# Five edits to a one-core hybrid-attention layer: later decays, a full-row decay product, spread x loads, a GpSimd subtract, and a shorter last layer norm

## The chip, the cores and the metric

The kernel runs on one core of a Trainium2 chip. The metric is the device time of one execution in microseconds (us), the median over several runs.

## What is computed

One residual block on x of 2048 tokens by 1024 channels, fp32:

```python
IN_SIZES = (DN_WIDTH, DN_WIDTH, DN_WIDTH,     # q, k, v of branch A, 4 heads of 128
            DN_WIDTH,                         # its gate z
            DN_HEADS, DN_HEADS,               # beta and decay, one per head and token
            SWA_WIDTH, SWA_KV_WIDTH, SWA_KV_WIDTH, SWA_WIDTH,   # branch B: 8 query heads, 2 kv heads of 64
            D_MODEL, D_MODEL)                 # the two merge gates
# A: S <- exp(g_t) S;  S <- S + k_t (beta_t (v_t - S^T k_t))^T;  o_t = S^T q_t   (gated delta rule)
g = jnp.cumsum(g, axis=-1)
decay = jnp.where(causal, jnp.exp(jnp.where(causal, g[..., :, None] - g[..., None, :], 0.0)), 0.0)
t_inv = lax.linalg.triangular_solve(eye + lower, eye)     # lower = strict(k_beta k^T * decay)
```

Branch B is attention over a window of 128 tokens with learned sinks and partial rotary embedding. Each branch is gated and projected to 1024 channels, the two are merged by sigmoid gates computed from x, projected once more, added to alpha times x, and normalized: (r - mean) * rsqrt(var + eps) * weight + bias.

## The kernel before, in words

The 2048 tokens go in 4 chunks of T = 512, one after the other. All dense products are fp32 made of two halves: `split` (L148) and `load_x` (L210) take a raw tile `w` from memory, ACT writes its rounded half hi (L160, L218) and DVE the rest lo = raw - hi (L161, L219), and `prods` issues three matmuls per product (L179, L180, L181). A split weight is used in all four chunks: chunk 0 splits it and SP writes the pair to a scratch tensor `kw_...` (`keep`, L145); later chunks load the pair (`wb<-kw_...`, L156). Two rings matter: the raw tiles `w` are three (W_RAW), shared by weights and x, and the pairs `wb` are four (W_SPLIT). x of a chunk lives in eight hi and eight lo tiles (`px`), which the last gate product of a chunk reads; the next chunk's x goes into the same tiles.

The first weights and x of chunk 0 have their own path in `start` (L224): ACT splits x (L235), DVE makes its lo (L236), and DVE casts each of six weight tiles (L241) and subtracts (L242).

Per chunk and head, branch A runs as generators that are put between the dense products: `decays` (per chunk: gates on DVE, two cumulative sums by matmul, L293 and L294, and a transpose of them whose result `GT` (8 rows by 512) ACT writes, L310), then `front` per head: a transpose of k (L369), the product that spreads head h's decay to 128 rows (L382, an 8-row selector `sel` against `GT`), the product k k^T (L393). Its masked blocks go to memory (`scrm`) and come back as `su`; `inverse` (L427) inverts 32 by 32 blocks on DVE (L943, L944), writes the result `xi` to `scrp` (L432), and `levels` (L434) reads it back in four loads into `p_` (L445), which PE needs at L457, then L464 after a transpose on DVE (L450). `back` (L482) runs the recurrence: L504, DVE L506, L509 and L512, DVE L511, L515 and L517, four times per head. Attention scores are L598 and L599; its query rows L606 to L616 lie on DVE and ACT.

PE's order is written out at build time by class `Order` (L829): `spawn(name, task, after)` lets a generator start `after` ns of counted PE work later, and each `yield cost, latency` puts its next step behind that much more. `decays` is spawned with LAT_Y = 8300 once the window's keys are through (L270). The other engines' queues are ordered by a scheduler that estimates when each operand is ready; so a change in PE's order also changes the order of SP's DMA issues and of DVE. Each queue runs strictly in its order.

After the dense list of a chunk comes `branch_b` for eight output tiles d (L653), each with a half weight `b{d}`, and ahead of it one call `load_x(nxt, KT - 1)` issues all eight x loads of the next chunk. After the last chunk `last_project` (L734) computes 128 tokens at a time; the norm of the last 128 tokens is the end of the program: `norm_factors` (L693), then per half of 512 channels a scale and shift (DVE L764 or ACT L762), a weight (DVE L765), a bias (POOL L766 for the first half, DVE L766 for the second), and the output DMA (L767).

Of the kernel before, what the change touches and what calls it, by code (L numbers as in the profile page):

```python
# [8 lines left out]
F32 = mybir.dt.float32  # L9
F32R = mybir.dt.float32r  # L10
AF = mybir.ActivationFunctionType
ALU = mybir.AluOpType
# [4 lines left out]
P = 128  # L17
D = 1024
KT = D // P
T = 512  # L20
NB = T // P
NH = 4
# [14 lines left out]

PE_R, PE_F, PE_T, PE_Q = 216, 218, 109, 45

LAT_INV, LAT_B, LAT_S, LAT_N, LAT_SM, LAT_D, LAT_M, LAT_K, LAT_Q, LAT_Y, LAT_F, LAT_W = 29600, 2700, 2300, 7700, 9200, 11000, 9000, 1400, 7900, 8300, 4100, 2300  # L40
FIRST = ("h01", "h00", "h02")


# [20 lines left out]
def build(tc, xt, xn, wk, wg, par, lnp, cst, out, seq=2048):  # L64
    nc = tc.nc
    NCH = seq // T
    with ExitStack() as ctx:
# [64 lines left out]

        selt = const.tile([8, NH], F32, name="selt")
        nc.sync.dma_start(out=selt, in_=cst[:8, C_SEL:C_SEL + NH])
        sel = const.tile([8, NH], F32R, name="sel")
        nc.vector.tensor_copy(sel, selt)
        ctx.enter_context(tc.manual_schedule(engines={mybir.EngineType.PE}))


# [83 lines left out]
        def start(c):  # L223

            ps = [pp.tile([P, T], F32, name="pp") for _ in range(2)] + [pd.tile([P, T], F32, name="pd")]

            idle = mm.tile([P, T], F32, name="mm")
            for _ in range(WARM):
                nc.tensor.matmul(idle, S[:, 0], S.rearrange("p h d -> p (h d)"), start=True, stop=True)
            for k in range(KT):  # L230
                if not k % 2:
                    hi, lo = (px.tile([P, 2, T], F32R, name=n) for n in ("xh", "xl"))
                    c.xh += [hi[:, 0], hi[:, 1]]
                    c.xl += [lo[:, 0], lo[:, 1]]
                nc.scalar.activation(c.xh[k], first[f"x{k}"], AF.Copy)  # L235
                nc.vector.tensor_tensor(c.xl[k], first[f"x{k}"], c.xh[k].bitcast(F32), ALU.subtract)  # L236
                if not k % 4:
                    wb = [pw.tile([P, 2, 528], F32R, name="wb", bufs=W_SPLIT)[:, :, :512] for _ in FIRST]
                    wh, wl = ([b[:, n] for b in wb] for n in range(2))
                    for i in range(3):  # L240
                        nc.vector.tensor_copy(wh[i], first[i + 3 * (k // 4)])  # L241
                        nc.vector.tensor_tensor(wl[i], first[i + 3 * (k // 4)], wh[i].bitcast(F32), ALU.subtract)  # L242
                        keep((FIRST[i], k // 4), wb[i])
                for i in range(3):
                    sl = slice(128 * (k % 4), 128 * (k % 4) + 128)
                    yield from prods(ps[i], [(wh[i][:, sl], wl[i][:, sl], c.xh[k], c.xl[k])], k == 0, k == KT - 1)
            for i, j in enumerate((1, 0, 2)):
                conv_silu(c, j, 0, ps[i])
            st.spawn("front0", front(c, 0), LAT_F)
# [35 lines left out]
        def decays(c, ba):  # L285
            c.beta, c.g = gates_small(nc, sm, ba, nea, prm[:, P_DTB:P_DTB + 4])
            flat = lambda a: a.rearrange("p b h -> p (b h)")
            new = lambda name: sm.tile([P, NB, NH], F32, name=name)
            c.nG, c.kd, c.neG, c.eGl = new("nG"), new("kd"), new("neG"), new("eGl")
            psg = pd.tile([P, T], F32, name="pd")  # L290
            tri = sm.tile([P, P], F32, name="wc", bufs=1)
            nc.vector.tensor_scalar(tri, dmask, 0.0, None, ALU.is_ge)
            nc.tensor.matmul(psg[:, :16], tri, flat(c.g), start=True, stop=True)  # L293
            nc.tensor.matmul(psg[:, 16:32], ones, flat(c.g), start=True, stop=True)  # L294
            G = psg[:, :16].rearrange("p (b h) -> p b h", h=NH)
            gg = sm.tile([P, NB, 2, NH], F32R, name="ghl", bufs=1)
            nc.vector.tensor_copy(gg[:, :, 0], G)
            nc.vector.tensor_tensor(gg[:, :, 1], G, gg[:, :, 0].bitcast(F32), ALU.subtract)
            nc.vector.tensor_scalar(flat(c.nG), psg[:, :16], -1.0, None, ALU.mult)
            nc.vector.tensor_tensor(flat(c.kd), psg[:, 16:32], flat(c.nG), ALU.add)  # L300
            nc.scalar.activation(c.kd, c.kd, AF.Exp)
            nc.scalar.activation(c.neG, c.nG, AF.Exp, scale=-1.0)
            nc.vector.tensor_scalar(c.neG, c.neG, -1.0, None, ALU.mult)
            nc.scalar.activation(flat(c.eGl), psg[:, 16:32], AF.Exp)
            yield 2 * 426, 2000
            psr = pd.tile([P, T], F32, name="pd")
            for b in range(NB):
                nc.tensor.transpose(tok(psr, b)[:8], gg[:, b].bitcast(F32).rearrange("p a h -> p (a h)"), ident)
            c.GT = sm.tile([8, T], F32R, name="GT", bufs=1)
            nc.scalar.activation(c.GT, psr[:8], AF.Copy)  # L310
            yield 4 * PE_T, 1000

        def conv_silu(c, j, h, ps):
# [42 lines left out]
        def front(c, h):  # L356
# [22 lines left out]
            yield 4 * PE_T, LAT_B  # L379

            psR = p4()
            nc.tensor.matmul(psR, sel[:, h:h + 1].to_broadcast([8, P]), c.GT, start=True, stop=True)  # L382
            dt = t4("dt", 2)
            for b in range(NB):
                nc.vector.scalar_tensor_tensor(dt[:, b], psR[:, b], c.nG[:, b, h:h + 1], dmask, ALU.add, ALU.add)
# [304 lines left out]
            for bp in range(2):  # L690
                nc.vector.scalar_tensor_tensor(c.ra[bp][:, :, es], xr[bp], 2.0 * ALPHA, pss[bp], ALU.mult, ALU.add)

        def norm_factors(c, bst, bufs=None):  # L693
            mv = sm.tile([P, 2], F32, name="mv", bufs=NB)
            nc.vector.bn_aggr(mv, bst)
            va = sm.tile([P, 1], F32, name="va")
            nc.vector.tensor_scalar(va, mv[:, 1:2], 4.0e-5, None, ALU.add)
            rs = sm.tile([P, 1], F32, name="rs", bufs=NB)
            rsqrt(nc, sm, rs, va, mhalf)
            if bufs:  # L700
                return rs, mv[:, 0:1]
            nm = sm.tile([P, 1], F32, name="lnm")
            nc.vector.scalar_tensor_tensor(nm, mv[:, 0:1], -1.0, rs, ALU.mult, ALU.mult)
            return rs, nm

        def layer_norm(c):
            fs = []
            for b in range(NB):
                r = c.ra[b // 2][:, b % 2]
                bst = sm.tile([P, 4, 6], F32, name="st", bufs=1)[:, :2]  # L710
                for i in range(2):
                    nc.vector.bn_stats(bst[:, i], r[:, 512 * i:512 * i + 512])
                rs, mu = norm_factors(c, bst, NB)
                fs.append((r, rs, mu))
                yield None, 2500
            for eg in range(4):
                es = slice(256 * eg, 256 * eg + 256)
                lg = pa.tile([P, 2, 256], F32, name="s")
                nc.sync.dma_start(out=lg, in_=bass.AP(tensor=lnp.tensor, offset=lnp.offset + 256 * eg, ap=[[0, P], [D, 2], [1, 256]]))
                for r, rs, mu in fs:  # L720
                    nc.vector.scalar_tensor_tensor(r[:, es], r[:, es], mu, lg[:, 0], ALU.subtract, ALU.mult)
                    nc.vector.scalar_tensor_tensor(r[:, es], r[:, es], rs, lg[:, 1], ALU.mult, ALU.add)
                    yield None, 1800
            for bp in range(2):
                t0 = c.i * T + bp * 256
                nc.sync.dma_start(out=out[t0:t0 + 256].rearrange("(b p) e -> p b e", p=P), in_=c.ra[bp])
# [7 lines left out]
        def last_project(c):  # L734
# [9 lines left out]
            for b in range(NB):  # L744
                r, t0 = ra[b // 2][:, b % 2], c.i * T + b * P
                bst = sm.tile([P, 4, 6], F32, name="st", bufs=1)
                for e0 in (0, 2):
# [7 lines left out]
                    for e, ps in enumerate(pss):  # L755
                        es = slice(256 * (e0 + e), 256 * (e0 + e) + 256)
                        nc.vector.scalar_tensor_tensor(r[:, es], xr[:, e], 2.0 * ALPHA, ps, ALU.mult, ALU.add)
                        nc.vector.bn_stats(bst[:, e0 + e], r[:, es])
                rs, nm = norm_factors(c, bst)
                for hs in (slice(0, 512), slice(512, D)):  # L760
                    if hs.start:
                        nc.scalar.activation(r[:, hs], r[:, hs], AF.Identity, scale=rs, bias=nm)  # L762
                    else:
                        nc.vector.tensor_scalar(r[:, hs], r[:, hs], rs, nm, ALU.mult, ALU.add)  # L764
                    nc.vector.tensor_tensor(r[:, hs], r[:, hs], lg[:, 0, hs], ALU.mult)  # L765
                    (nc.vector if hs.start else nc.gpsimd).tensor_tensor(r[:, hs], r[:, hs], lg[:, 1, hs], ALU.add)  # L766
                    nc.sync.dma_start(out=out[t0:t0 + P, hs], in_=r[:, hs])  # L767

        class Chunk:
# [26 lines left out]
        for i in range(NCH):  # L796
# [7 lines left out]
                    piece(c, w)  # L804
            for name in ("window0", "window1"):
                st.finish(name)
            if i < NCH - 1:
                load_x(nxt, KT - 1)
            for d in range(KT):
                st.dense([branch_b(c, d)])  # L810
            if i < NCH - 1:
                for w, first_done in EARLY:
                    st.finish(first_done)
                    if w == "q0":
                        st.done -= early_done - {"decay", "kT0", "kT1", "kT2", "kT3"}
                    nxt.early.add(w)
                    piece(nxt, w)
# [202 lines left out]
```

## Time and profile before

| | us |
|---|---|
| median of 3 runs (1693.77 to 1695.6) | 1695.29 |
| the profiled execution | 1688.99 |
| its span | 1687.2 |
| PE busy | 1619.6 (96%) |
| DVE busy | 976.0 (58%) |
| ACT busy | 600.8 (36%) |
| POOL busy | 88.9 (5%) |

The profiled execution is 6.3 us under the median and has 1.8 us around its span. PE is at work almost all the time, so time can be lost only where PE waits, where a matmul takes longer than it must, or where the granted clock of PE is below 1.00 (0.50 is the lower of its two levels, 1.2 GHz of 2.4). Waits of other engines count only if PE stands behind them. Later times are counted from the start of the span.

### The profile page before, as it was taken

How to read it: one execution, taken by the hardware profiler on the slowest of the kernel's cores; microseconds unless marked ns; L12 is line 12 of the kernel's file. 1: busy time of each engine (PE TensorE's matmuls, PEld its weight loads, DVE VectorE, ACT ScalarE, POOL GpSimd, SP SyncE). 2: the span in 40 equal slices, each digit the busy share in tenths (PEclk: the TensorE clock that was granted, in tenths of full speed). 3: DMA queues.
4: the chain of work that ended last, by engine and by line, in shares of the span. 5: the costliest groups of instructions: out<-in, count | busy, mean ns of one | idle time of the engine just before them, and what ended most of it. 6: DMA issues, size and time to landing. Idle time of an engine off the chain costs nothing.

```text
span 1687.2 us, 26971 instructions
## 1 busy us (share of the span) xinstructions
PE 1619.6 (96%) x9846; PEld 1366.6 (81%) x9846; DVE 976.0 (58%) x3015; ACT 600.8 (36%) x1692; POOL 88.9 (5%) x138
## 2 busy tenths in 40 slices
PE   9999999899899999999999999999999999999997
PEld 6878877787788778788888778878888878888787
DVE  6676686548748665433746774623482867462255
ACT  4464456424313633432311453333230244233110
POOL 0100000000001001000000000000000100000001
PEclk9999999999989999999999999999999999999999
DMA  8866584676857446556655835645656664464862
GB/s 307 265 223 198 180 272 154 207 237 218 280 199 221 133 145 176 157 146 224 197 178 182 245 120 150 178 144 176 207 176 193 221 185 122 149 197 138 285 207 76
DMA packets 189157, 323.37 MB, mean 192 GB/s; under 512 B 31072, under 2 KB 45408, under 8 KB 188896
## 3 DMA queue, kind: packets, MB, share of 16 engines
q1 hardware_dynamic: 185184, 316.40, 59.3%
q0 software_dynamic: 3840, 5.25, 1.5%
q8 instruction: 78, 1.28, 0.3%
q14 instruction: 55, 0.45, 0.1%
HBM read 244.97 MB, written 71.37 MB: 187 GB/s over the span
## 4 chain that ended last, share of the span: by engine, by line
PE 79%; DMA 8%; DVE 8%; ACT 2%; issue 1%; SPq 1%; POOL 0%; DVEq 0%; ACTq 0%
PE mm L179 22%; PE mm L181 21%; PE mm L180 21%; PE pp L633 2%; DMA s<-in_lnp 2%; PE pp L625 1%; DMA wb<-kw_o 1%; DMA w<-in_wg 1%; DMA wb<-kw_zb 1%; PE pp L598 1%; PE pd L509 1%; PE pd L504 1%; PE pd L393 1%; PE pp L599 1%; DMA wb<-kw_b 1%
## 5 line engine op out<-in xcount | busy, mean ns | idle before, releaser
L179 PE MATMUL mm<-xh,wb 128*128 128x512 f32 x1128 | 467.1, 414 | 2.0 <-DMA wb<-kw_zb 1.6
L181 PE MATMUL mm<-xh,wb 128*128 128x512 f32 x1128 | 445.4, 395 | 0.0
L180 PE MATMUL mm<-xl,wb 128*128 128x512 f32 x1128 | 444.2, 394 | 0.0
L179 PEld LDWEIGHTS mm<-xh,wb 128*128 128x128 f32 x1128 | 213.1, 189 | 50.3 <-issue 8.9
L181 PEld LDWEIGHTS mm<-xh,wb 128*128 128x128 f32 x1128 | 212.3, 188 | 49.9
L180 PEld LDWEIGHTS mm<-xl,wb 128*128 128x128 f32 x1128 | 213.8, 190 | 38.0
L179 PE MATMUL mm<-wb,xh 128*128 128x256 f32 (+1 forms) x384 | 115.1, 300 | 3.2 <-DVE rope L893 2.9
L179 PE MATMUL mm<-wb,s 128*128 128x256 f32 x384 | 112.1, 292 | 5.5 <-DMA wb<-kw_o 5.3
L180 PE MATMUL mm<-wb,xh 128*128 128x256 f32 (+1 forms) x384 | 109.1, 284 | 0.0
L181 PE MATMUL mm<-wb,s 128*128 128x256 f32 x384 | 109.0, 284 | 0.0
L180 PE MATMUL mm<-wb,s 128*128 128x256 f32 x384 | 108.9, 284 | 0.0
L181 PE MATMUL mm<-wb,xl 128*128 128x256 f32 (+1 forms) x384 | 108.6, 283 | 0.0
L161 DVE TENSOR_TENSOR wb<-w,wb 128x512 fp32r<-128x512 f32 (+1 forms) x110 | 75.7, 690 | 56.2 <-ACT wb L160 53.9
L160 ACT ACTIVATE wb<-w 128x512 fp32r<-128x512 f32 (+1 forms) x110 | 68.9, 628 | 84.8 <-PE mm L181 47.2
L179 PEld LDWEIGHTS mm<-wb,s 128*128 128x128 f32 x384 | 73.6, 192 | 8.3 <-DMA wb<-kw_o 5.2
L943 DVE TENSOR_TENSOR xt<-su,xi 128x16 f32<-128x16 f32 (+15 forms) x256 | 76.4, 298 | 5.4
L179 PEld LDWEIGHTS mm<-wb,xh 128*128 128x128 f32 x384 | 73.2, 191 | 5.8 <-issue 5.4
L944 DVE TENSOR_REDUCE xi<-xt 128x8 f32<-128x16 f32 (+15 forms) x256 | 74.8, 292 | 5.1
L611 ACT ACTIVATE s<-s,nm 128x256 f32<-128x256 f32 (+1 forms) x128 | 62.6, 491 | 39.8 <-DVE nm L608 39.8
L180 PEld LDWEIGHTS mm<-wb,s 128*128 128x128 f32 x384 | 73.6, 192 | 0.1
L181 PEld LDWEIGHTS mm<-wb,s 128*128 128x128 f32 x384 | 73.5, 192 | 0.0
L317 ACT ACTIVATE xs<-mm 128x512 f32<-128x512 f32 x45 | 26.8, 596 | 131.0 <-PE mm L181 129.7
(665 smaller groups left out, 3045.6 us busy)
## 6 DMA issues: line engine op xcount, KB each, us to landing
wb<-kw_h SPq DMA_DIRECT2D x96, 512.0 KB, 4.1
wb<-kw_g SPq DMA_DIRECT2D x96, 512.0 KB, 3.9
w<-in_wg SPq DMA_DIRECT2D x106, 256.0 KB, 4.1
wb<-kw_b SPq DMA_DIRECT2D x48, 512.0 KB, 4.1
wb<-kw_o SPq DMA_DIRECT2D x36, 512.0 KB, 4.5
kw_h<-wb SPq DMA_DIRECT2D x32, 512.0 KB, 3.9
kw_g<-wb SPq DMA_DIRECT2D x32, 512.0 KB, 3.4
wb<-kw_q SPq DMA_DIRECT2D x24, 512.0 KB, 3.9
```

The source lines that it names most:

```text
L160: nc.scalar.activation(hi, raw, AF.Copy)
L161: nc.vector.tensor_tensor(lo, raw, hi.bitcast(F32), ALU.subtract)
L179: nc.tensor.matmul(ps, sh, mh, start=(first and i == 0), stop=False)
L180: nc.tensor.matmul(ps, sh, ml, start=False, stop=False)
L181: nc.tensor.matmul(ps, sl, mh, start=False, stop=(last and i == n))
L317: nc.scalar.activation(xs[:, 3:], ps, AF.Copy)
L393: nc.tensor.matmul(psKK[:, b], k4[:, b], k4[:, b], start=True, stop=True)
L504: nc.tensor.matmul(ps, k4[:, b], S[:, h], start=True, stop=True)
L611: nc.scalar.activation(ss[v][:, g, k0:], ss[v][:, g, k0:], AF.Exp, bias=nm[:, v, g:g + 1], scale=0.125, accum_out=su[:, v, g:g + 1])
L633: nc.tensor.matmul(psY[64 * v:64 * v + 64], c.vs[b + kb][:, 64 * v:64 * v + 64], pTs[v][:, kb], start=(kb == kbs[0]), stop=(kb == 1))
L943: nc.vector.tensor_tensor(tx[:, :, :, :n], u, x, ALU.mult)
L944: nc.vector.tensor_reduce(xi[:, :, i:i + 2], tx[:, :, :, :n], AX.X, ALU.add)
```

## The change

Five edits. (1) LAT_Y goes from 8300 to 11500, so `decays` comes later in PE's order, and with it all that waits for it. (2) `sel` and `GT` become constant tiles of 128 rows, filled with zeros once by POOL, of which 8 rows are written as before; the decay product (L382) runs over 128 rows instead of 8. (3) In `start` the six subtracts L242 go from DVE to POOL. (4) The next chunk's x loads are called one at a time, behind each `branch_b`, instead of all eight ahead of the first. (5) The last layer norm takes two passes per half, both on DVE, (r - mean) * weight and then * rs + bias, instead of scale and shift, weight and bias on ACT, DVE and POOL; the small operation for -mean * rs (L703) falls away. Lines of the kernel after are three or four higher up to `norm_factors`, three lower behind the norm's edits.

```diff
-LAT_INV, ..., LAT_Y, LAT_F, LAT_W = 29600, ..., 8300, 4100, 2300
+LAT_INV, ..., LAT_Y, LAT_F, LAT_W = 29600, ..., 11500, 4100, 2300
...
-        sel = const.tile([8, NH], F32R, name="sel")
-        nc.vector.tensor_copy(sel, selt)
+        sel = const.tile([P, NH], F32R, name="sel")
+        GT = const.tile([P, T], F32R, name="GT")
+        for t in (sel, GT):
+            nc.gpsimd.memset(t.bitcast(F32), 0.0)
+        nc.vector.tensor_copy(sel[:8], selt)
...
                         nc.vector.tensor_copy(wh[i], first[i + 3 * (k // 4)])
-                        nc.vector.tensor_tensor(wl[i], first[i + 3 * (k // 4)], wh[i].bitcast(F32), ALU.subtract)
+                        nc.gpsimd.tensor_tensor(wl[i], first[i + 3 * (k // 4)], wh[i].bitcast(F32), ALU.subtract)
...
-            c.GT = sm.tile([8, T], F32R, name="GT", bufs=1)
-            nc.scalar.activation(c.GT, psr[:8], AF.Copy)
+            nc.scalar.activation(GT[:8], psr[:8], AF.Copy)
...
-            nc.tensor.matmul(psR, sel[:, h:h + 1].to_broadcast([8, P]), c.GT, start=True, stop=True)
+            nc.tensor.matmul(psR, sel[:, h:h + 1].to_broadcast([P, P]), GT, start=True, stop=True)
...
-                rs, nm = norm_factors(c, bst)
-                for hs in (slice(0, 512), slice(512, D)):
-                    if hs.start:
-                        nc.scalar.activation(r[:, hs], r[:, hs], AF.Identity, scale=rs, bias=nm)
-                    else:
-                        nc.vector.tensor_scalar(r[:, hs], r[:, hs], rs, nm, ALU.mult, ALU.add)
-                    nc.vector.tensor_tensor(r[:, hs], r[:, hs], lg[:, 0, hs], ALU.mult)
-                    (nc.vector if hs.start else nc.gpsimd).tensor_tensor(r[:, hs], r[:, hs], lg[:, 1, hs], ALU.add)
+                rs, mu = norm_factors(c, bst)
+                halves = slice(0, 512), slice(512, D)
+                for hs in halves:
+                    nc.vector.scalar_tensor_tensor(r[:, hs], r[:, hs], mu, lg[:, 0, hs], ALU.subtract, ALU.mult)
+                for hs in halves:
+                    nc.vector.scalar_tensor_tensor(r[:, hs], r[:, hs], rs, lg[:, 1, hs], ALU.mult, ALU.add)
                     nc.sync.dma_start(out=out[t0:t0 + P, hs], in_=r[:, hs])
...
-            if i < NCH - 1:
-                load_x(nxt, KT - 1)
             for d in range(KT):
                 st.dense([branch_b(c, d)])
+                if i < NCH - 1:
+                    load_x(nxt, d)
```

What moves is best seen in the engines' rows. The first place is head 1 of chunk 0, where PE reads the inverted blocks `p_` (L457 before, L460 now). Before, PE:

```order
L179 MATMUL mm<-xh,wb 128x512
L180 MATMUL mm<-xl,wb 128x512
L181 MATMUL mm<-xh,wb 128x512
L515 MATMUL pd<-wc,ktl 128x128
L517 MATMUL pd<-wc,dt 128x128
L457 MATMUL pd<-p__1855,m_1486 32x32
```

Now, PE:

```order
L183 MATMUL mm<-xh,wb 128x512
L184 MATMUL mm<-xl,wb 128x512
L185 MATMUL mm<-xh,wb 128x512
L512 MATMUL pd<-bt,q__1040 128x128
L515 MATMUL pd<-S,qd 128x128
L460 MATMUL pd<-p__1870,m_1477 32x32
```

PE now comes to it one half of a recurrence step earlier (twelve dense matmuls and the pair L515, L517, which stood ahead of it and now follow). At the same place SP before (`kw_h` are the keeps of weights just split, `scrp` takes the inverse, `p_` reads it back):

```order
L145 DMA kw_h_0_2031<-wb 256x1x512
L159 DMA w<-in_wg 128x512
L432 DMA scrp_151<-xi 128x128
L145 DMA kw_h_1_2064<-wb 256x1x512
L445 DMA p__1855<-scrp_151 32x4x32 x4
```

Now, SP:

```order
L149 DMA kw_h_1_2066<-wb 256x1x512
L163 DMA w<-in_wg 128x512
L149 DMA kw_h_0_2102<-wb 256x1x512
L163 DMA w<-in_wg 128x512
L435 DMA scrp_151<-xi 128x128
L149 DMA kw_h_1_2136<-wb 256x1x512
L448 DMA p__1870<-scrp_151 32x4x32 x4
```

The write of the inverse stands two weights further back in SP's queue; one keep is between it and the reads, as before.

The second place is SP around `branch_b` of chunk 0 (`in_xt` is x, `kw_b` and the `w` beside it the weights of `branch_b`, all by the ring of three). Before:

```order
L145 DMA kw_g_0_3696<-wb 256x1x512
L217 DMA w<-in_xt 128x512
L145 DMA kw_g_1_3729<-wb 256x1x512
L217 DMA w<-in_xt 128x512 x6
L159 DMA w<-in_wg 128x512 x3
L145 DMA kw_b_1_3795<-wb 256x1x512
L159 DMA w<-in_wg 128x512
L145 DMA kw_b_1_3821<-wb 256x1x512
```

Now:

```order
L149 DMA kw_g_0_3698<-wb 256x1x512
L221 DMA w<-in_xt 128x512
L149 DMA kw_g_1_3731<-wb 256x1x512
L163 DMA w<-in_wg 128x512
L149 DMA kw_b_1_3757<-wb 256x1x512
L221 DMA w<-in_xt 128x512
L149 DMA kw_b_1_3789<-wb 256x1x512
L163 DMA w<-in_wg 128x512
L221 DMA w<-in_xt 128x512
L163 DMA w<-in_wg 128x512
L149 DMA kw_b_1_3818<-wb 256x1x512
```

The weights of the first two branches no longer stand behind x; from the third on, one x tile and one weight alternate in the ring. In chunks 1 and 2, where weights come as pairs, the order of the x loads is as before.

The third place is SP at head 0 of chunk 1 (`kw_o` keeps of the output projection's weights, `s<-in_xn` the residual input). Before:

```order
L145 DMA kw_o_1_5044<-wb 256x1x512
L432 DMA scrp_150<-xi 128x128
L159 DMA w<-in_wg 128x512
L687 DMA s<-in_xn 128x2x256
L145 DMA kw_o_0_5080<-wb 256x1x512
L687 DMA s<-in_xn 128x2x256
L159 DMA w<-in_wg 128x512
L145 DMA kw_o_1_5099<-wb 256x1x512
L445 DMA p__4900<-scrp_150 32x4x32 x4
```

Now:

```order
L435 DMA scrp_150<-xi 128x128
L149 DMA kw_o_0_5026<-wb 256x1x512
L163 DMA w<-in_wg 128x512
L149 DMA kw_o_1_5045<-wb 256x1x512
L448 DMA p__4901<-scrp_150 32x4x32 x4
L690 DMA s<-in_xn 128x2x256 x2
L149 DMA kw_o_0_5081<-wb 256x1x512
```

The reads of `p_` now stand right behind the keep that stood ahead of `scrp` before, and ahead of the residual loads and two keeps.

## Rows read from the trace of the kernel before

**Rows 1.** The page: busy time, share of the span and instructions of each engine.

```profile
PE 1619.6 (96%) x9846; PEld 1366.6 (81%) x9846; DVE 976.0 (58%) x3015; ACT 600.8 (36%) x1692; POOL 88.9 (5%) x138
```

**Rows 2.** Waits of PE: what it waited for, us in total, times, longest.

```profile
PE pd L457 <- DMA p__4900<-scrp: 8.4, 1, 8.4
PE mm L179 <- ACT wb L160: 7.2, 1, 7.2
...
PE pd L464 <- DVE q__968 L450: 3.6, 1, 3.6
PE mm L179 <- DVE rope L893: 2.9, 1, 2.9
...
PE pd L293 <- DVE gg L922: 2.6, 1, 2.6
PE pd L457 <- DMA p__2747<-scrp: 2.4, 1, 2.4
```

**Rows 3.** Windows: us, busy time of each engine, PEclk, DMA share, GB/s.

```profile
48.00:52.00 4.00, 3.92 (x24) 3.96 (x25) 3.35 (x22) 1.68 (x7) 1.02 (x2) 0.69 1.02 365
...
124.00:128.00 4.00, 4.00 (x20) 3.48 (x17) 1.75 (x7) 2.47 (x9) 0.00 (x0) 0.57 0.03 4
...
336.00:344.00 8.00, 3.81 (x11) 3.01 (x12) 3.13 (x6) 3.15 (x5) 0.00 (x0) 0.57 0.71 219
388.00:396.00 8.00, 5.41 (x31) 4.22 (x29) 6.18 (x17) 3.13 (x10) 0.00 (x0) 1.00 0.74 234
...
464.00:472.00 8.00, 5.98 (x40) 5.79 (x41) 1.51 (x5) 0.27 (x1) 0.00 (x0) 0.50 0.21 60
```

**Rows 4.** Timeline of PE, 405 to 408 us: start, us, line, out<-in.

```profile
405.99 0.39 PE L181 MATMUL mm<-yAh,wb 128*128 128x512 f32 x1
406.31 0.49 PE L382 MATMUL pd<-GT,sel 8*128 8x512 f32 x1
406.73 0.51 PE L179 MATMUL mm<-yAh,wb 128*128 128x512 f32 x1
407.08 0.39 PE L180 MATMUL mm<-yAl,wb 128*128 128x512 f32 x1
```

**Rows 5.** Timeline of DVE in `start`, 5 to 21 us.

```profile
9.13 1.29 DVE L242 TENSOR_TENSOR wb<-s,wb 128x512 fp32r<-128x512 f32 x2
...
18.98 0.69 DVE L242 TENSOR_TENSOR wb<-s,wb 128x512 fp32r<-128x512 f32 x1
```

**Rows 6.** Timeline of the end, 1678.9 us on, all engines.

```profile
1679.25 0.16 DVE L703 SCALAR_TENSOR_TENSOR lnm<-mv,rs 128x1 f32<-128x1 f32 x1
...
1680.03 1.29 DVE L765 TENSOR_TENSOR yBl<-yBl,yAh 128x512 f32<-128x512 f32 x2
1680.80 1.64 POOL L766 TENSOR_TENSOR yBl<-yBl,yAh 128x512 f32<-128x512 f32 x1 [2.17 <-DVE yBl L765]
1681.35 1.63 DVE L766 TENSOR_TENSOR yBl<-yBl,yAh 128x512 f32<-128x512 f32 x1
```

**Rows 7.** Timeline of SP, then PE, at head 1 of chunk 0.

```profile
163.45 0.33 SPq L432 DMA_DIRECT2D scrp<-xi  x1
...
166.69 1.76 SPq L445 DMA_DIRECT2D p__1855<-scrp  x4
...
170.58 0.21 PE L457 MATMUL pd<-p__1855,m 32*32 32x32 f32 x1
```

**Rows 8.** Timeline of SP at `branch_b` of chunk 0, and a row of DMA issues.

```profile
323.13 12.63 SPq L217 DMA_DIRECT2D w<-in_xt  x6
336.03 4.46 SPq L159 DMA_DIRECT2D w<-in_wg  x3
...
w<-in_wg SPq DMA_DIRECT2D x106, 256.0 KB, 4.1
```

**Rows 9.** Timeline of SP at head 0 of chunk 1.

```profile
454.77 0.58 SPq L432 DMA_DIRECT2D scrp<-xi  x1
...
460.77 2.75 SPq L445 DMA_DIRECT2D p__4900<-scrp  x4
```

More of the change, by code (lines that the diff above doesn't have):

```diff
@@ L38 @@
 PE_R, PE_F, PE_T, PE_Q = 216, 218, 109, 45
-LAT_INV, LAT_B, LAT_S, LAT_N, LAT_SM, LAT_D, LAT_M, LAT_K, LAT_Q, LAT_Y, LAT_F, LAT_W = 29600, 2700, 2300, 7700, 9200, 11000, 9000, 1400, 7900, 8300, 4100, 2300
+LAT_INV, LAT_B, LAT_S, LAT_N, LAT_SM, LAT_D, LAT_M, LAT_K, LAT_Q, LAT_Y, LAT_F, LAT_W = 29600, 2700, 2300, 7700, 9200, 11000, 9000, 1400, 7900, 11500, 4100, 2300
 FIRST = ("h01", "h00", "h02")
@@ L691, in project, with norm_factors @@
                 nc.vector.scalar_tensor_tensor(c.ra[bp][:, :, es], xr[bp], 2.0 * ALPHA, pss[bp], ALU.mult, ALU.add)
-        def norm_factors(c, bst, bufs=None):
+        def norm_factors(c, bst):
             mv = sm.tile([P, 2], F32, name="mv", bufs=NB)
@@ L699, in norm_factors @@
             rsqrt(nc, sm, rs, va, mhalf)
[L700 to L704, printed above, removed]
+            return rs, mv[:, 0:1]
         def layer_norm(c):
@@ L712, in layer_norm @@
                     nc.vector.bn_stats(bst[:, i], r[:, 512 * i:512 * i + 512])
-                rs, mu = norm_factors(c, bst, NB)
+                rs, mu = norm_factors(c, bst)
                 fs.append((r, rs, mu))
@@ L758, in last_project @@
                         nc.vector.bn_stats(bst[:, e0 + e], r[:, es])
-                rs, nm = norm_factors(c, bst)
-                for hs in (slice(0, 512), slice(512, D)):
-                    if hs.start:
-                        nc.scalar.activation(r[:, hs], r[:, hs], AF.Identity, scale=rs, bias=nm)
-                    else:
-                        nc.vector.tensor_scalar(r[:, hs], r[:, hs], rs, nm, ALU.mult, ALU.add)
-                    nc.vector.tensor_tensor(r[:, hs], r[:, hs], lg[:, 0, hs], ALU.mult)
-                    (nc.vector if hs.start else nc.gpsimd).tensor_tensor(r[:, hs], r[:, hs], lg[:, 1, hs], ALU.add)
+                rs, mu = norm_factors(c, bst)
+                halves = slice(0, 512), slice(512, D)
[3 more added lines that the diff above has]
+                    nc.vector.scalar_tensor_tensor(r[:, hs], r[:, hs], rs, lg[:, 1, hs], ALU.mult, ALU.add)
                     nc.sync.dma_start(out=out[t0:t0 + P, hs], in_=r[:, hs])
```

## The prediction

> **What bounds the kernel.** I read the page first: PE is busy 96% of the span, 1619.6 us [rows 1], and no other engine comes near. So time can come from three places only: PE's waits, the granted clock, and matmuls that take longer than their neighbours. The list of PE's waits [rows 2] gives the first: six waits, each occurring once, make 27 us, and all six stand at places that this change reorders. The windows [rows 3] give the second: the granted clock is 1.00 almost throughout, but 0.50 to 0.69 after four of those waits, and I price a low stretch as PE's busy time in it times what is missing of 1.00. In 464 to 472 us that is 5.98 x 0.50 = 3.0 us; 1.2 in 48 to 52, 1.7 in 124 to 128, 1.6 in 336 to 344. The wait of 2.6 us for `gg` in 388 to 396 left the clock at 1.00, so a wait much under 3 us seems to cost its own length alone. The timeline of PE around the decay product [rows 4] gives the third.
>
> The sum stands against the profiled execution (span 1687.2, 1688.99 with what lies around it). That one was 6.3 us quicker than the median of 1695.29; I take the difference over to the median unchanged. A measurement of this kernel can tell about 0.2%, 3.4 us, from no change.
>
> **Part by part.**
>
> *Start, +1.2.* Two subtracts together took 1.29 us on DVE and the last one 0.69 [rows 5]; the only two-input operation of that size on POOL took 1.64 [rows 6]. If POOL began the pair when DVE did, its end would be 3.28 - 1.29 = 2.0 later. POOL is however not held up by the casts and x's lows that share DVE, so it begins the second one earlier: I take +1.2. In the second half of the weights the last subtract gains 1.64 - 0.69 = 1.0 of length, but PE is already that much later, so this does not add. Below: -0.3, as x's lows come sooner on a freer DVE; above: +2.5. The two zero fills lie on POOL ahead of this; nothing there is late yet. The Trainium skill (SBUF - State Buffer, section Who interferes with whom) says that a DVE instruction with two SBUF inputs and a GpSimd one that reads SBUF lock each other out for a whole instruction. The pair at the end agrees: DVE's addition took 1.63 beside POOL's and half of 1.29 without [rows 6]. By that rule the DVE's casts and lows also stop beside each subtract, and the term would be nearer its upper bound.
>
> *Wait of 2.9 for the rotary rows, chunk 0, -3.3.* The rotary row stood on DVE behind a weight split that waited for its raw tile. In the changed order of DVE the rotary rows and the copy beside them stand ahead of that split. With the low clock behind it (1.2) the place cost 4.1; I leave 0.8 of a wait, for the matmuls that the rows themselves come from. Bounds 0 and -4.1.
>
> *Head 0, L464, -4.7.* PE reached L464 3.6 us (and another 0.4) ahead of DVE's transpose L450, which stood behind the decay factors and attention rows of the same head. LAT_Y moves `decays` 3.2 us of counted work back, so PE comes to L457 and L464 about 5 us of its work later, behind more dense products. DVE's transpose still has attention rows ahead of it, so I leave 1 us: 3.6 + 0.4 + 1.7 of clock - 1.0. Bounds -2 and -5.7.
>
> *Head 1, L457, +9.* This is the price of the same edit. Before, the inverse was written at 163.45, read at 166.69 to 168.45, and PE came at 170.58 without a wait [rows 7]: 7.1 us from the inverse to use. The inverse now begins some 3.7 us of PE work later, since the last work of head 0 does, while PE comes to L457 half a recurrence step earlier. Placed against the third L504 of head 0 (at time T): the inverse ends at T+2.8 on DVE, since two weight splits and L506 stand between its last passes; 7.1 later it is T+9.9; PE arrives at T+3.5, after twelve dense matmuls at 0.23 (the distance of full-row neighbours in [rows 4], less the decay product). That is 6.3 of wait. Then L464 and L509 follow directly on their producers instead of behind dense work, +0.7, and the clock falls for about 2 (between 1.2 and 3.0 [rows 3]). What is queued behind: the keep that stands between `scrp` and `p_` on SP must issue first, so a late weight delays PE too. Bounds +4 and +12.
>
> *Head 2, +2.* PE waited 2.4 there already [rows 2]; the loads now stand behind one more keep, about 2 us. Bounds 0 and +4.
>
> *`branch_b` of chunk 0, -4.5.* Six x loads held SP for 12.63 us, because each needs a free raw tile, and the first weights of `branch_b` came behind them at 336.03 [rows 8]: PE waited 7.2, and 1.6 of clock came on top: 8.8. Now the first two weights go ahead of x. From the third on x and weights alternate in a ring of three, so a new weight comes every two turns of the ring: 4.1 from issue to landing [rows 8], some 1.3 for ACT and DVE, under 1 to issue, shared by three tiles, 2 x 6.3 / 3 = 4.2 us per branch where PE needs 2.8 (12 x 0.23). Over the eight that makes waits up to 1.4 x 6 = 8, less what x and weights gain by being issued ahead of time; I take 4.3. Each such wait is short, so I charge no clock. Bounds 0 and -8.8.
>
> *`gg` in chunk 1, -2.6.* L293 now comes 4 us of PE work later and the wait of 2.6 [rows 2] goes; what follows it is not nearer. Bounds -1 and -2.6.
>
> *Head 0 of chunk 1, -6.* PE waited 8.4 for `p_` [rows 2]. The inverse was written at 454.77 but the reads issued only from 460.77 and took 2.75 [rows 9], behind residual loads and two keeps. In the change they stand ahead of these, so only the landing of the write holds them: at head 1 that was 3.2 from issue to issue [rows 7], which gives 458 instead of 460.8, and 1.76 for the four instead of 2.75: 3.8 sooner, and a little more where DMA is less full. The wait is then about 4, and I take half of the 3.0 of clock back: 4.4 + 1.5. Bounds -3 and -11.4.
>
> *The decay product, -4.8.* From the matmul ahead of L382 to the second one behind it: 407.08 - 405.99 = 1.09 us, for three steps that take 0.23 each among full-row products, so 0.40 above. If the gaps come from changing between 8 and 128 rows they go, 16 times (4 chunks, 4 heads), 6.4; if from the product's place and its operands, nothing. I take 0.30 each, as other small full-row products keep a longer first step behind them. Bounds 0 and -6.4.
>
> *Last norm, -1.1.* From 1679.25, where L703 stood, four DVE passes at half of 1.29 make 1679.25 + 2.6 = 1681.85, against the end of DVE's last addition at 1681.35 + 1.63 = 1682.98 [rows 6]. POOL, which held that addition up, is out. Bounds -0.5 and -1.4. The norms of earlier tokens lie beside matmuls and cost nothing; the cover would go only if DVE (58% [rows 1]) came late there.
>
> Chunks 2 and 3 shift by one or two us of PE work with their loads' order unchanged: 0, give or take 1. **Sum:** 1.2 - 3.3 - 4.7 + 9 + 2 - 4.5 - 2.6 - 6 - 4.8 - 1.1 = -14.8: 1674 for the profiled execution, **1680.5** against the median.
>
> **Rivals.**
>
> *The scratch loads turn the sign.* At each of heads 1 to 3 of chunk 0 `p_` stands on SP behind a keep, which waits for ACT and DVE to split a weight. If that split ends more than 4 us after the inverse, each head costs what chunk 1's cost before, 8.4 + 3.0 = 11.4. Three of these in place of 9 + 2 make -14.8 + 34.2 - 11 = +8.4: 1703.7. It turns slower once the three heads cost 26 us together. For it: that is how the wait of 8.4 came about [rows 9]. Against: at heads 2 and 3 the order is nearly that of before, and head 2's cost 2.4.
>
> *The full-row product buys nothing.* Then only -10.0 is left: 1685.3. The Trainium skill (TensorE: Matmul & The Clock Gate, section Why this matters for your kernels) states that a single matmul of 32 rows takes the same time as one of 128, which speaks for this rival; the 0.40 us in [rows 4] speak against, but do not say which of its causes it has.
>
> *`branch_b` is bound by its ring.* If the eight weights all wait behind x (8 x 1.4 = 11 in place of the 8.8 that went), the term is +2.2 instead of -4.5: 1687.2. For it: six x loads took 12.63 us of SP [rows 8]. Against: the first two weights are ahead.
>
> **How the numbers follow.** My forecast 0.60; the full-row rival 0.14; the ring 0.13; the scratch loads 0.13. The forecast with its bounds (mainly head 1 and chunk 1, some 6 us either way, and `branch_b`) spans 1671 to 1690; the second and third rivals lie in that. I set the range to 1669 to 1697, which leaves out the worst of the scratch loads and the best of all bounds at once. Faster by over 0.2% (under 1691.9): 0.60 less 0.02, 0.13 of the full-row rival, 0.07 of the ring: 0.78. Within: 0.10, from the ring and mild scratch waits. Slower: 0.12.
>
> **What would show it.** In the waits of the changed kernel: L179 on the rotary rows and on ACT's split at `branch_b` much smaller, `gg` of chunk 1 gone, L460 (the old L457) at head 1 of chunk 0 new with about 6 us and a low clock behind it, chunk 1's about 4. L385 (the old L382) should be followed at 0.23 by its neighbours, and the last DVE pass end 2.6 us behind the first. I am wrong if L460 waits at several heads of chunk 0, or if `branch_b` still waits over 7.

## The result, and the profile after

The changed kernel takes **1673.26 us** (median of 6 runs, 1671.39 to 1680.04) against 1695.44 for the kernel before in the same comparison (6 runs, 1691.99 to 1700.42): ratio **0.9875, 95% interval 0.9850 to 0.9899**, or 21 us less (17 to 25). Faster, as forecast, inside the range of 1669 to 1697, and 7 us better than the 1680.5 that stood as the likeliest.

The page of the changed kernel, busy time by engine (compare [rows 1]):

```profile
span 1675.8 us, 26955 instructions
...
PE 1618.4 (97%) x9846; PEld 1368.5 (82%) x9846; DVE 972.9 (58%) x3005; ACT 598.1 (36%) x1688; POOL 92.7 (6%) x142
```

PE's work is what it was (1.2 us less); the time came from its pauses. But the two profiled executions differ by only 11.4 us of span, half of what the medians say; that half is a question of its own, taken up below. PE's waits (compare [rows 2]), columns as there:

```profile
PE mm L183 <- DMA wb<-kw_o: 5.9, 9, 1.0
PE pd L507 <- DVE S L519: 5.4, 4, 1.8
PE pd L460 <- DMA p__1870<-scrp: 5.1, 1, 5.1
PE pd L512 <- DVE bt L509: 4.4, 4, 1.8
PE pd L460 <- DMA p__2749<-scrp: 3.2, 1, 3.2
...
PE pd L460 <- DMA p__4901<-scrp: 2.8, 1, 2.8
...
PE mm L183 <- DVE q__12942 L453: 2.0, 1, 2.0
...
PE pd L185 <- POOL wb L246: 1.5, 2, 1.1
PE mm L183 <- DVE kr L892: 1.0, 1, 1.0
...
PE mm L183 <- DVE rope L890: 0.8, 1, 0.8
```

Of the six long waits of before, three are gone: `branch_b`'s 7.2 on ACT, L464's 3.6, the gates' 2.6. Two are small (rotary rows 2.9 to 0.8, chunk 1's blocks 8.4 to 2.8). One grew, head 2's from 2.4 to 3.2, and one is new: 5.1 at head 1 of chunk 0, `p__1870`. Shorter waits are new too, among them 2.0 in chunk 3, for `q__12942`, and 1.0 at the key rows L892. Windows of the changed kernel, columns as in [rows 3]:

```profile
48.00:52.00 4.00, 4.00 (x36) 4.00 (x35) 3.69 (x22) 1.43 (x8) 1.02 (x2) 1.00 1.06 385
124.00:128.00 4.00, 4.00 (x30) 3.32 (x29) 1.47 (x4) 2.96 (x13) 0.19 (x1) 1.00 0.68 161
168.00:172.00 4.00, 3.46 (x42) 2.85 (x38) 1.61 (x6) 0.80 (x3) 0.00 (x0) 0.50 0.24 75
172.00:176.00 4.00, 4.00 (x25) 3.32 (x23) 0.73 (x3) 1.39 (x7) 0.72 (x2) 0.50 0.00 0
176.00:180.00 4.00, 4.00 (x12) 3.22 (x13) 2.23 (x11) 0.46 (x4) 1.01 (x1) 0.50 0.00 0
...
336.00:344.00 8.00, 8.00 (x41) 6.74 (x40) 3.19 (x6) 2.15 (x4) 0.00 (x0) 1.00 0.66 210
384.00:392.00 8.00, 8.00 (x39) 6.52 (x38) 7.53 (x25) 4.33 (x10) 0.82 (x2) 1.00 0.73 228
456.00:464.00 8.00, 7.64 (x80) 7.32 (x81) 1.80 (x7) 0.80 (x3) 0.00 (x0) 0.79 0.76 262
...
1276.00:1280.00 4.00, 4.00 (x35) 3.71 (x34) 0.30 (x1) 0.27 (x1) 0.00 (x0) 0.57 0.76 266
```

At 48, 124 and 336 the clock is at 1.00 where it was 0.69, 0.57 and 0.57 [rows 3], and PE is busy throughout; the low stretch now lies behind the new wait at 167, at 0.50 for over 11 us: 0.5 x (3.46 + 4 + 4) = 5.7 us, more than the wait itself. Over the whole span the two profiled executions were granted nearly the same clock, 0.989 before and 0.990 now, so their 11.4 us are shorter pauses on balance: the span less PE's busy time is 67.6 us before and 57.4 now.

How far ahead the changed kernel is in the two traces (start after minus start before; lines as in the kernel before). The rows that count matmuls compare points where both kernels have done the same ones. A single line can mislead where the order has changed: the first L625, at 92 us, comes 4.1 us sooner, while the dense matmuls around it come 2.6 sooner.

| at | before, us | after minus before |
|---|---|---|
| behind the first 156 matmuls, ahead of the rotary rows | 39 | +1.4 |
| behind the first 233, after the rotary rows | 53 | -2.2 |
| behind the first 710, behind head 0's L464 | 139 | -8.3 |
| L625, behind head 1 | 239 | +1.6 |
| head 3's L492, behind head 2 | 328 | +4.0 |
| L541, behind `branch_b` | 389 | -1.0 |
| L382, chunk 1 head 0 (gates) | 406 | -4.0 |
| L492, chunk 1 (blocks read) | 486 | -11.0 |
| L625, end of chunk 2 | 1158 | -11.3 |
| last L541 | 1581 | -9.3 |
| last matmul | 1676 | -8.5 |
| end of span | 1687.2 | -11.4 |

Most of the 2.0 us lost between 1158 and 1581 lie in chunk 3: behind the wait for `q__12942` the clock is 0.57 from 1276 to 1280 us, 0.43 x 4.00 = 1.7.

### The profile page after: what moved, and what is told of

Read it like the earlier page. It is cut to its first block, busy times and chain, and to the rows that moved or that the text cites. A ratio compares the mean times of both kernels' runs of the same rounds, so it can differ in the third digit from the quotient of the medians.

```text
span 1675.8 us, 26955 instructions
## 1 busy us (share of the span) xinstructions
PE 1618.4 (97%) x9846; PEld 1368.5 (82%) x9846; DVE 972.9 (58%) x3005; ACT 598.1 (36%) x1688; POOL 92.7 (6%) x142
## 4 chain that ended last, share of the span: by engine, by line
PE 80%; DMA 9%; DVE 7%; ACT 2%; SPq 1%; issue 1%; POOL 0%; DVEq 0%; ACTq 0%
PE mm L183 22%; PE mm L185 21%; PE mm L184 21%; DMA s<-in_lnp 2%; PE pp L636 2%; DMA wb<-kw_o 1%; PE pp L628 1%; DMA scrp<-xi 1%; PE pp L601 1%; PE pp L602 1%; PE pd L422 1%; DMA w<-in_xt 1%; PE pd L396 1%; DMA wb<-kw_b 1%; PE pd L507 1%
```

## The experiments

All runs below are timed in rounds with the kernel before on the same chip (11 to 28 executions of it, medians 1695.1 to 1697.2), and so compared by ratio. The changed kernel's is 0.9875.

**The kernel before, again** (no edit).

> The kernel before, once more, against itself. Its profiled execution was 6.3 us under its median and that of the changed kernel 4.4 us over its own, so the two profiles differ by 11.4 us where the medians differ by 22.2. Theory one (executions scatter, by waits on transfers that vary): the time is the same within 0.2%, a new profile lies anywhere between 1688 and 1700, and its long waits (8.4 for the scratch blocks of chunk 1, 7.2 at branch_b, 3.6 at L464) differ by some us each from those seen. Theory two (the profiled execution was of another kind): the new profile is near 1695 with the same waits, and 6 us are found somewhere else.

0.9986 (0.9965 to 1.0006), its profile the quickest of its own 12 executions: 1689.77, median 1694.02. The long waits are those of before within 0.4 us (8.0, 7.1, 3.8, 3.0, 2.6 and 2.4), so it is not transfers that differ. What differs is the clock behind them. Windows of this execution:

```profile
48.00:52.00 4.00, 3.20 (x27) 3.23 (x28) 3.58 (x23) 1.63 (x8) 0.53 (x2) 1.00 1.07 375
124.00:128.00 4.00, 4.00 (x14) 3.52 (x15) 1.50 (x6) 1.99 (x6) 0.00 (x0) 0.50 0.01 2
388.00:396.00 8.00, 5.41 (x28) 4.31 (x28) 7.09 (x21) 3.98 (x11) 0.00 (x0) 1.00 0.87 262
```

The rotary wait was 3.0 here and 2.9 in [rows 2], yet the clock stayed at 1.00 at 48 us where it had fallen to 0.69. Each execution also carries its mean granted clock: over 28 executions of before it runs from 0.980 (1706.71 us) to 0.988 (1692.12), about 1.7 us for each 0.001 by a straight line (0.8 to 1.7 in the three smaller sets further down); the profiled execution of before had 0.989, above all of these, and the six of the changed kernel have 0.990 or 0.991. Neither theory held whole: the new profile's time lies in the span of theory one, the waits are the same as in theory two, and neither looked at the clock. Nor is it luck alone that the profiled execution was quick: it lies under all three executions of its own run, and in six of the twelve runs here the profiled execution is the quickest of its run (that of the changed kernel is the fifth of six). Why is not known.

**Without both reorderings.** LAT_Y 8300, x loads in one run; the full-row product, GpSimd's subtracts and the short norm stay.

```diff
-LAT_Y = 11500
+LAT_Y = 8300
...
+            if i < NCH - 1:
+                load_x(nxt, KT - 1)
             for d in range(KT):
                 st.dense([branch_b(c, d)])
-                if i < NCH - 1:
-                    load_x(nxt, d)
```

> The changed kernel with LAT_Y back at 8300 and the x loads back in one run ahead of branch_b: the full-row product, the subtracts on GpSimd and the short norm alone. By the profiles the full-row product gives about 0.4 us at three of four heads (4 to 5 in all), the norm 1 to 2, the start costs up to 1: about 1689 against 1695.4, with the waits of 8.4 at chunk 1 and 7 at branch_b as before. Rival, that PE only comes earlier to the next wait: within 0.2% of before.

0.9956 (0.9935 to 0.9976), 7.5 us less than before, in line with the 6 expected. Its trace has the old waits, of the chunk's blocks and of the gates:

```profile
PE pd L460 <- DMA p__4901<-scrp: 8.3, 1, 8.3
...
PE pd L297 <- DVE gg L919: 3.1, 2, 2.6
```

The rotary wait, however, is 0.8, as in the changed kernel. And this time the gates' 2.6, which left the clock at 1.00 in both traces of before, was followed by a low stretch:

```profile
392.00:396.00 4.00, 1.59 (x6) 1.50 (x7) 3.87 (x11) 1.51 (x4) 0.00 (x0) 0.75 0.90 292
396.00:400.00 4.00, 4.00 (x11) 3.13 (x10) 0.44 (x4) 0.50 (x3) 0.00 (x0) 0.50 0.32 92
```

**Later decays alone**, on the kernel before.

```diff
-LAT_Y = 8300
+LAT_Y = 11500
```

> The kernel before with LAT_Y 11500 and nothing else. In the order of SP this alone moves the reads of the inverted blocks at chunk 1 ahead of two keeps. Theory: about -5 at L464 of head 0, -3 at the gates of chunk 1, -7 at chunk 1's scratch blocks, +10 and +2 at heads 1 and 2 of chunk 0, perhaps -3 at the rotary rows: -3 to -7, 1688 to 1692. Rival, that the new wait at head 1 outweighs it: 1698 or more.

0.9937 (0.9916 to 0.9958): 10.7 us less. The profiled execution, 1683.17, is 5.8 under that of before, inside the -3 to -7 worked out for the profiles; the medians again show more. The rival fell. The new wait at head 1 is there (4.9), chunk 1's blocks fell to 2.6, the rotary wait of 2.7 stayed: that one is not the work of LAT_Y.

**The changed kernel without the spread x loads.**

```diff
+            if i < NCH - 1:
+                load_x(nxt, KT - 1)
             for d in range(KT):
                 st.dense([branch_b(c, d)])
-                if i < NCH - 1:
-                    load_x(nxt, d)
```

> The changed kernel with the eight x loads again ahead of branch_b. Theory: a wait of about 7 us at branch_b of chunk 0 with a low clock comes back, less the 3.4 us that the recurrence behind it waits in the changed kernel: 5 us more, 1678; the scratch blocks of chunk 1 keep their earlier place and their wait of under 3. Rival, that the waits behind branch_b stay: 8 to 9 us more, 1682. If spreading x did nothing: 1673.

0.9900 (0.9869 to 0.9931), median 1679.80: 4 us worse than the changed kernel by ratio, but the two intervals overlap. In the traces the wait of 7.2 at `branch_b` is back and PE falls behind the changed kernel by 5.2 us over that stretch, near the 5 expected; chunk 1's blocks stay at 2.5. By the end of the span this trace has made it up again (1675.4 against 1675.8), since it lacks the low stretches at 456 and 1276 us and has smaller waits.

**The changed kernel without the later decays.**

```diff
-LAT_Y = 11500
+LAT_Y = 8300
```

> The changed kernel with LAT_Y back at 8300, the rest kept (x still spread, which by itself keeps the reads of chunk 1's scratch blocks early). Theory: the 5.1 and 3.2 us of waits at heads 1 and 2 of chunk 0 and most of their low clock go (-10), the 3.6 at L464 and its clock come back (+5.5), so does the wait of 2.6 for the gates of chunk 1 with a chance of a low clock (+3 to 4): about 1672, no slower than the changed kernel at 1673.3. Rival, that later decays carry the gain as their own run (10.7 faster than before) suggests: 1680 or more.

0.9892 (0.9875 to 0.9909), median 1676.54. Between the two theories: 3 us worse by ratio, inside the changed kernel's interval, so the time does not tell the two apart. The trace shows the trade as expected, no wait for head 1's blocks, and in return:

```profile
PE pd L467 <- DVE q__970 L453: 4.0, 1, 4.0
PE pd L460 <- DMA p__2749<-scrp: 3.4, 1, 3.4
PE pd L297 <- DVE gg L919: 2.8, 2, 2.6
...
PE pd L460 <- DMA p__4901<-scrp: 2.7, 1, 2.7
```

The last row matters: chunk 1's blocks were early **without** the later decays, too. The four runs make a square (us of 1695 by ratio, the other three edits in all of them):

| | x in one run | x spread |
|---|---|---|
| LAT_Y 8300 | -7.5 (blocks 8.3) | -18.3 (blocks 2.7) |
| LAT_Y 11500 | -17.0 (blocks 2.5) | -21.2 (blocks 2.8) |

Separately the two edits give 9.5 and 10.8, together 13.7: 6.6 would be counted once only. Each ratio is good to 3 to 5 us, and so this difference of differences to some 8: the times alone do not show it. The waits do: chunk 1's is 8.3 in one cell and 2.5 to 2.8 in the three others, so either edit takes it away. Beside the spread x loads the later decays are not shown to add anything.

**The decay product over 8 rows again.**

```diff
-            nc.tensor.matmul(psR, sel[:, h:h + 1].to_broadcast([P, P]), GT, start=True, stop=True)
+            nc.tensor.matmul(psR, sel[:8, h:h + 1].to_broadcast([8, P]), GT[:8], start=True, stop=True)
```

> The changed kernel with the decay product over 8 rows again (same constant tiles). Theory: gaps of 0.32, 0.42 and 0.34 us instead of 0.23 around three of four products per chunk, the fourth waits for DVE anyway: 12 x 0.35 = 4 us more, 1677.5. Rival, that gaps only shift into waits: 1673.

0.9882 (0.9866 to 0.9897), median 1677.11: 3.8 us by the medians, but the intervals overlap, so the time does not settle it. The traces show the price at the place. PE around the product, first the changed kernel, then this one:

```profile
402.12 0.39 PE L185 MATMUL mm<-yAh,wb 128*128 128x512 f32 x1
402.34 0.40 PE L385 MATMUL pd<-GT,sel 128*128 128x512 f32 x1
402.57 0.40 PE L183 MATMUL mm<-yAh,wb 128*128 128x512 f32 x1
402.81 0.40 PE L184 MATMUL mm<-yAl,wb 128*128 128x512 f32 x1
```

```profile
402.02 0.39 PE L185 MATMUL mm<-yAh,wb 128*128 128x512 f32 x1
402.34 0.49 PE L385 MATMUL pd<-GT,sel 8*128 8x512 f32 x1
402.76 0.50 PE L183 MATMUL mm<-yAh,wb 128*128 128x512 f32 x1
403.10 0.40 PE L184 MATMUL mm<-yAl,wb 128*128 128x512 f32 x1
```

The steps of 0.32, 0.42 and 0.34 become 0.22, 0.23 and 0.24 at the same place: 0.39 us are the price of the eight rows. At head 3 of chunks 1 to 3 it is as much, at head 2 it is 0.33. At head 1 of chunks 1 to 3 it is given back, since there PE waits for DVE's `ktl` (0.58 to 1.14 us before, 0.91 to 1.16 after). The prices do not add up, though: at L544 behind chunk 2, 1161 us, past twelve such products, this execution is 0.3 us behind the changed kernel, and its span is the shorter by 1.1. So the price is shown where the product stands, not at the end; the rival, that gaps shift into waits, stays open.

**Blocks later, LAT_D 14000 and 17000** (from 11000).

```diff
-LAT_D = 11000
+LAT_D = 14000
```

> The changed kernel with LAT_D 14000 instead of 11000: PE comes to the inverted blocks (L460) twelve dense matmuls later at heads 1 and 2 of chunk 0, and SP reads them right behind the write at head 1. Theory: the wait of 5.1 at head 1 falls to 2 or less and that of 3.2 at head 2 to under 1, with most of the low clock behind them (some 6 and 3 in the profile); the recurrence steps stand closer and give back 2: about -10, 1663. Rival, that what waits is the recurrence itself: within 3 us of 1673.

> The same with LAT_D 17000: another recurrence step ahead of L460. Theory: no wait for the blocks is left, but four steps of the recurrence stand with nothing between them at head 1 and wait for DVE: 2 to 4 us worse than with 14000, about 1666. Rival, the more room the better: 1660.

Both missed: 0.9911 (median 1682.13) and 1.0062 (1707.99). With 14000, head 1 still waits 3.5 and head 2 now 3.0 at L476; with 17000 head 1's blocks cost only 1.3 and 0.9 in chunk 0, but the next step of an inverse, L467, waits 7.7 at head 1 of chunks 1 to 3 and 7.3 at head 2 of chunk 0, and the recurrence (L512) waits more:

```profile
PE pd L512 <- DVE bt L509: 11.9, 9, 2.4
PE pd L467 <- DVE q__13936 L453: 7.7, 1, 7.7
PE pd L467 <- DVE q__9812 L453: 7.7, 1, 7.7
PE pd L467 <- DVE q__5688 L453: 7.7, 1, 7.7
```

By the code nothing dense lies there in chunk 0's written order: `k2` may start only when head 0's recurrence is done (the `finish` in `head_in`), so chunk 0 drains it without cover, whatever the latencies say. The next run tests this. What makes L453 late in chunks 1 to 3 was not followed.

**A gate ahead of `k2`.**

```diff
-ORDER_FIRST = "... z0 v1 g z1 k2 q2 v2 w1 k3 g q3 g v3 g g g g z2 z3 g g"
+ORDER_FIRST = "... z0 v1 g z1 g k2 q2 v2 w1 k3 g q3 g v3 g g g z2 z3 g g"
```

> The changed kernel with one of the sixteen merge gates of chunk 0 (24 dense matmuls, 5.5 us of PE) moved in the written order from behind v3 to ahead of k2, so that PE has dense work while head 0's recurrence is drained and head 1's blocks are fetched. Theory (the wait of 5.1 at L460 of head 1 is there because nothing dense is left to put in between): it falls to 2 or less, the low clock behind it (some 6 us in the profile) mostly goes: 8 us less, 1665; the end of chunk 0 may wait 1 to 2 more. Rival, that the blocks come later by as much: 1673.

Half right. Head 1's wait fell as expected, so it was dense work that was missing there, but the time is the same, 0.9871 (0.9851 to 0.9892), median 1673.27. Waits for the blocks:

```profile
PE pd L460 <- DMA p__4862<-scrp: 4.3, 1, 4.3
...
PE pd L460 <- DMA p__2790<-scrp: 2.7, 1, 2.7
...
PE pd L460 <- DMA p__1870<-scrp: 1.6, 1, 1.6
```

Chunk 1's (`p__4862`) went from 2.8 to 4.3. Where both have done the same matmuls, PE's lead over the changed kernel is 7.9 us at 440 us, about the 8 expected, and 0.6 at 699: the gain is eaten in chunk 1. Part of it goes to the clock. Between 546 and 554 us PE stops four times, for 0.3 to 1.3 us, and the clock falls (columns as above):

```profile
552.00:556.00 4.00, 2.73 (x36) 2.53 (x37) 1.73 (x3) 2.86 (x8) 0.19 (x1) 0.71 0.45 131
556.00:560.00 4.00, 4.00 (x20) 3.05 (x20) 2.80 (x9) 3.18 (x12) 1.08 (x1) 0.50 0.01 2
```

In the changed kernel the clock is at 1.00 in both windows. The rest was not followed further.

**Later decays only from chunk 1 on.**

```diff
-            st.spawn("decay", decays(c, ba), LAT_Y)
+            st.spawn("decay", decays(c, ba), LAT_Y if c.i else 8300)
```

> The changed kernel with LAT_Y 8300 in chunk 0 and 11500 in chunks 1 to 3. Theory (the later decays gain at the gates of chunk 1 and lose at head 1 of chunk 0): chunk 0 as with 8300 everywhere, 3.8 us sooner at its end by that profile, and no wait of 2.6 with its low clock at chunk 1: 1669 to 1670. Rival, that the whole kernel shifts with the order: 1673 or more.

0.9860 (0.9836 to 0.9883), median 1672.33. In its trace PE is 3.1 us ahead of the changed kernel at the end of chunk 0 and 3.8 at the end of chunk 2, as the theory said; in time that is not to be told from it.

**Subtracts back on DVE.**

```diff
-                        nc.gpsimd.tensor_tensor(wl[i], first[i + 3 * (k // 4)], wh[i].bitcast(F32), ALU.subtract)
+                        nc.vector.tensor_tensor(wl[i], first[i + 3 * (k // 4)], wh[i].bitcast(F32), ALU.subtract)
```

> The changed kernel with the six first subtracts back on DVE. Theory: PE's waits for GpSimd's lows in the first 21 us (0.6, 1.1, 0.4 in the profile, 2.1 in all, against 0.5 before) go: 1 to 1.5 us less, 1672, at the edge of what can be told. Rival, that the freed DVE is worth more (the rotary rows' wait of 2.9 fell to 0.8 in the same stretch): 1675 or more, with that wait longer.

0.9858 (0.9836 to 0.9879), median 1671.89: no difference that can be told. The waits of both theories show at once, that for GpSimd is gone and the rotary wait is back, but the 3 us that the rival put on it did not come:

```profile
PE mm L183 <- DVE rope L890: 3.3, 1, 3.3
...
PE pp L185 <- DVE wb L246: 1.0, 1, 1.0
```

So it is this edit, not the later decays, that put the rotary rows ahead of the weight split: by moving DVE's own order. The two runs with LAT_Y alone (2.7) and without it (0.8) agree. That the edit gains time on the whole is not shown.

**Three edits together**: LAT_Y 8300 in chunk 0, the gate ahead of `k2`, and in chunk 0's head 0 `yield 8 * PE_Q, LAT_B + 4000` between L460 and L467.

> Three edits on the changed kernel, to see whether it can be beaten: LAT_Y 8300 in chunk 0, the gate moved ahead of k2, and L467 of head 0 of chunk 0 put 4 us of counted PE work behind its producer (the wait of 4.0 with a low clock behind it that the 8300 brings back). Theory: no wait over 2 us before 240 us, so 4 to 6 us less than with 8300 in chunk 0 alone (1672.3): 1667. Rival, that a removed wait comes back at the next place, as when the gate alone was moved: 1672 to 1674.

As the rival has it, and 4 us above it: 0.9885 (0.9858 to 0.9912), median 1677.64. L467's 4.0 fell to 0.7, and 3.3 at head 2 and 3.7 at chunk 1 are left. No version beat the changed kernel beyond the noise.

## Why the prediction was right, and where its sizes were off

*Start, +1.2.* Up to the rotary rows PE waited 3.5 instead of 2.3: +1.2, but for another reason in part. The weights cost 2.5 instead of 2.0, +0.5; the rest is the wait of 1.0 at the key rows L892 (0.3 there before), which the prediction did not name, so its size is partly luck. The subtracts on POOL took 1.27 to 1.76, and DVE's cast beside one 1.32 instead of 0.42:

```profile
8.32 1.32 DVE L245 CAST wb<-s 128x512 fp32r<-128x512 f32 x1 [0.32 <-DMA s<-in_wg]
```

```profile
9.71 1.76 POOL L246 TENSOR_TENSOR wb<-s,wb 128x512 fp32r<-128x512 f32 x1 [0.36 <-DVE wb L245]
```

The rule that the prediction took from the Trainium skill (SBUF - State Buffer, section Who interferes with whom), in the words that it gave, is about DVE instructions with two SBUF inputs. It agrees with x's low L240, which took 1.58 us at 6.08 beside a subtract and 0.69 without; the cast has one input, and those words do not cover it.

*Rotary rows, -3.3:* the wait went from 2.9 to 0.8 and the low clock went, -3.6 by the table, and start and rotary rows together -2.2 against -2.1. The cause is shown by the run with the subtracts back. *Head 0, -4.7:* 4.0 to 0.4 of wait and 1.7 of clock, -5.3; -6.1 by the table, with two decay products and other small gains in it. *Head 1, +9:* the wait is 5.1 + 0.3, not 6.3, but the clock cost 5.7, not 2: +9.9 by the table. *Head 2, +2:* +2.4. *`branch_b`, -4.5:* -5.0, by another route: none of the 4.3 us left for the ring came, since the weights were on time, but the recurrence behind it now waits (L507 1.8, L512 1.6). *Gates, -2.6:* -3.0. *Chunk 1's blocks, -6:* -7.0. *Norm, -1.1:* -2.9 by the table, from the last matmul on; 1.8 of that is DVE, from `va` to the end of its last pass (5.1 to 3.4), and 1.1 lie behind it and were not followed. The prediction started all four passes at 1679.25, when rs was known; the first two need only the mean and run while POOL is at rs:

```profile
1669.43 1.40 DVE L761 SCALAR_TENSOR_TENSOR yBl<-yBl,mv,yAh 128x512 f32<-128x512 f32 x2
1669.60 0.98 POOL L875 TENSOR_TENSOR rs<-va,mhalf 128x1 f32<-128x1 f32 x1 [10.14 <-DVE va L700]
...
1671.33 1.41 DVE L763 SCALAR_TENSOR_TENSOR yBl<-yBl,rs,yAh 128x512 f32<-128x512 f32 x2
```

*Decay product, -4.8:* the price of 0.39 is shown at its place, so the mechanism that the rival doubted is there. The rule of the Trainium skill that 32 rows take the time of 128 (TensorE: Matmul & The Clock Gate, section Why this matters for your kernels) does not hold here: the measurement decides, a product of 8 rows between full ones cost 0.39 more. But the sum of -4.8 is not seen. From 486 to 1158 us, with seven products, the lead grows by 0.3, and the run with eight rows ends no later in its trace. So the rival's time, that the product buys nothing, is not refuted.

*Chunks 2 and 3, 0 give or take 1:* chunk 2 agrees, chunk 3 lost 2.0.

The scratch-load rival fell: heads 2 and 3 paid 3.7 and 0.4, not 11.4. So did the ring.

**The step that was mis-sized** is "I take the difference over to the median unchanged". The terms made -14.8 and the profiles show -11.4, but the medians moved by 22 (21 by ratio). That the forecast came within 7 us is in part luck: the terms were 3.4 better than the traces, and the step to the median left out 10.8.

The sum priced each wait by the clock that followed it in one execution, and that execution had one of the mildest clocks seen: 0.989, where of 73 other executions of the kernel before two had 0.989 or 0.990 and the rest 0.980 to 0.988. The sentence "a wait much under 3 us seems to cost its own length alone" rested on one draw; in another run the same 2.6 us was followed by 0.75 and 0.50. A wait of 2.5 to 3 us was followed by a low stretch in some traces and by none in others, so it has no fixed price. The change took away the waits for the rotary rows, at L464, at `branch_b` and for the gates, shortened chunk 1's, and added those at head 1 and in chunk 3.

Some 4 to 9 of the 21 us are then the clock: its mean rose by some 0.005, at 0.8 to 1.7 us per 0.001. That part is an estimate from the slopes; no run held the clock and changed the waits, and no trace shows an execution of the kernel before at its usual 0.985, so where the clock falls in it is not known. The profile of the changed kernel lies 4.4 us above its own median at nearly the same clock (0.990 against 0.990 or 0.991); that stays open.

## What to carry to other kernels

Where PE is busy 96% of the time, a pause of a few us costs its length plus, in some executions, as much again at half clock: price it from several executions, and let the mean granted clock of each say whether the profiled one was typical. Two edits can remove the same wait, and then it must not be counted twice: the waits in a square of four runs show that, the edits' own runs do not. Compare two traces only at points where both have done the same work; where the order has changed, one line's lead can be 1.5 us off. Here a wait in a written order was covered only by dense work that may stand there; with the waiting instruction pushed later (17000), the wait came back at its successor. A price shown at its place (0.39 us) need not reach the end.

## What was not expected of the hardware

One 8-row matmul between 128-row ones costs 0.39 us, in the step before it and the two behind it. And a stop of 2.6 to 3.0 us lowers PE's granted clock in one execution and not in the next: 1.00 or 0.69 at 48 us in two executions of the same kernel, and 1.00 or 0.50 behind the gates, there in two kernels. Over 28 executions of one kernel the mean clock goes with most of the spread from 1692 to 1707 us.
